# Moving the last pair's products ahead of the first inverse's products, and the bonus product to ScalarE, in a four-layer streaming encoder

## The chip, the core and the metric

The kernel runs on one core of a Trainium2 chip. A core has a matrix engine (TensorE, PE in the profile; its weight loads are shown as PEld), a vector engine (VectorE, DVE), an activation engine (ScalarE, ACT), a general engine (GpSimd, POOL) and a queue engine (SyncE, SP). Each takes its instructions in order from a queue of its own, and they wait for one another through semaphores. Matrix products land in PSUM, eight banks of 128 x 512 fp32; everything else lives in SBUF. The metric is the device time of one execution in microseconds (us).

## The reference, cut to what matters

Two residual layers, each followed by a gated convolutional FFN. The first mixes tokens by spatial gating, the second by an RWKV-7 recurrence. The change lies in the second mixer alone.

```
D, S, H, N = 1024, 512, 16 heads, 64 per head
r, k, v = xr @ w_r, xk @ w_k, xv @ w_v            # 512 x 1024 each
g = sigmoid(xg @ g1) @ g2
y = wkv7_scan(r, decay, k, v, -kk, kk * a)         # S_t = S diag(w) + (S a) b^T + v k^T ; y_t = S_t r_t
y = groupnorm_per_head(y) * ln_w + ln_b
bonus = sum(r * k * r_k, per head) * v
out = ((y + bonus) * g) @ w_o
```

The recurrence is computed in chunks of 64 positions. Inside a chunk it needs the inverse of a unit triangular 64 x 64 matrix for each head.

## The kernel before, in words

Activations lie as [128 channels, 512 positions] tiles, eight of them for the 1024 channels. A dense product with a 1024 x 1024 weight runs in fp32r with operands split into a high and a low part: three matmuls of 128 x 512 for each pair of a weight tile and an input tile (`mm3`, lines 325 to 327). `dense_steps` gives two input tiles, that is six matmuls, between two yields.

The heads come as eight **pairs** p = 0 to 7 of 128 channels, in two **groups** of four. Pairs 0 to 3 are group 0, pairs 4 to 7 group 1. `rwkv_main` consists of Python generators that emit instructions a bit at a time, and `weave` interleaves them:

- `pairs()` is the main stream of the first half. For each pair it emits `decay` (two pairs ahead), `operands` (one pair ahead) and `products`. `products` multiplies the pair's operands chunk by chunk into banks `aux` and `us` (L973, two halves; L988), VectorE masks them (L977), ScalarE copies parts into `ti` (L978) and `bt` (L991). A pair takes three main steps.
- `invert(g)` inverts the triangular blocks of a group. It copies and transposes them (ScalarE L1046 or VectorE L1044, VectorE L1051), runs a chain of 30 elimination steps j on VectorE (L1062 to L1070, each step on the result of the one before), transposes back (L1051 twice), and joins the blocks by small 32 x 32 matmuls (L1090, L1093) into bank `e` (group 0) or `aux` (group 1), which ScalarE copies out (L1098, L1103, L1105). It has 25 yields: one after the first transposes, fifteen in the chain, one after the transposes back, eight among the matmuls.
- `fill` is the stream of matrix work that keeps TensorE busy: `projections()` (keys, then values V0 to V7, four dense steps each), `gates()`, `project()` (the output product, first with group 0, then with group 1).
- `scan(g)` is the main stream of the second half: eight chunks of group g, three main steps each (L1301/L1305, L1314, L1321/L1326), whose matmuls wait for VectorE copies and sums between them. `finish` normalises what two chunks gave (ScalarE square L1342, VectorE L1347, GpSimd power L389, VectorE L1357, transposes by TensorE L1363, VectorE L1366).

The value stream is what the change touches most. After the four dense steps of pair m, ScalarE copies the bank to tile `v` (L854; one buffer). During the dense steps of pair m + 1, `value(m, v)` emits the centring transposes (L868) and later the **bonus**: a matmul of r*k with ones scaled by r_k (L883) into a bank, VectorE multiplies that bank by `v` into `rt` (L885), ScalarE adds the bias `ln_b` in place (L886). While pairs are still running, the dense accumulators, the transposes and the bonus share tag `mm`, which has two banks.

`weave(main, side, fill, rate, lag, side_rate)` takes one main step after another; after each it adds `side_rate` to the side's account and `rate` to the fill's, and takes as many whole steps of each as are due. A fill step may be issued no earlier than TensorE's last instruction of `lag` main steps ago. The order of the work is that of emission, with a planner that lays out each engine's queue ahead of time: among instructions that it takes to be ready, the one emitted first goes first. VectorE's elimination steps are tied to nothing but their operands, so they are put wherever VectorE is free; the inverse's matmuls are tied behind the last TensorE instruction (`step`).

Lines 1422 to 1440 set the order of the stretch around the change: pairs 0 to 3 with fill; pairs 4, 5, 6 with `invert(0)` at 2.2 steps a main step and fill at 1.9 (nine main steps; 19 side and 17 fill steps, and one more fill step inside `invert(0)`, L1077); then the last two main steps of pair 7 with `invert(0)` at 2.2 and fill at 1.2 (4 side, 2 fill steps); then what is left of `invert(0)` (one yield), with a fill step and a step of `ahead = invert(1)` for each yield; one fill step; `scan(0)` with the rest of `invert(1)` at 1.15 and fill at 0.66; `scan(1)` with fill at 0.72; and a written-out end (lines 1444 to 1454).

`gates()` takes `idle()` steps, two matmuls on constants (L1124) whose result nobody reads, as fill until group 0's last chunks are normalised (`normed`, L1177); two of them are taken in `scan(1)`. `gate` multiplies the finished `rt` by the gate in PSUM (L1209), and splits the result into the operands of the output product (L1213, L1214). After the last main step of `scan(1)` four dense steps of group 0's output product are left, m = 6 and 7; they lie among the normalisation of the last chunks, the gate's products (L1201) and the transposes L1363, ahead of the first product with group 1.

Of the kernel before, what the change touches and what calls it, by code (L numbers as in the profile page):

```python
# [12 lines left out]
F32 = mybir.dt.float32  # L13
F32R = mybir.dt.float32r
AF = mybir.ActivationFunctionType
ALU = mybir.AluOpType
# [4 lines left out]
P = 128  # L21
D = 1024
KT = 8
T = 512
# [5 lines left out]
GN_EPS = 64e-5  # L30
C1 = -0.5 * math.exp(-0.5)

RATES = ((1.9, 2), (1.9, 6, 2.2), (0.66, 2, 1.15), (0.72, 2), (1.2, 6, 2.2))
LEAD = 1
WB = 4
FIRST0, WAIT, STEPS = 1, 1, (2, 2, 2, 2)
# [108 lines left out]
class Emit:  # L145
# [622 lines left out]
    def rwkv_main(self, r, ctx, gain):  # L768
        nc, tc, A = self.nc, self.tc, self.A
        V, S, G = nc.vector, nc.scalar, nc.gpsimd  # L770
# [5 lines left out]
        ip = r.ip  # L776
# [31 lines left out]
        def projections():  # L808

            load = Ahead([lambda n=n, m=m: self.parts(n, m) for n in PARTS for m in range(KT)])  # L810

            def key(m, a):
                while m >= NKEY and m - NKEY not in used:
                    yield
                ks[m] = tmp("key", NKEY, T)
                S.copy(ks[m], a)

            for m in range(KT - 2):
                a = self.acc("mm")
                yield from self.dense_steps(a, load.take(), r.xk)  # L820
                yield from key(m, a)
                yield

            ws = [load.take(), load.take(False)]
            accs = [self.acc("mm") for _ in range(2)]
            xv = []
            for k in range(KT):
                for j in range(2):
                    self.mm3(accs[j], self.wcols(ws[j], k * P, P), r.xk[k], k == 0, k == KT - 1)
                while len(xv) < min(k + 3, KT):  # L830
                    xv.append(r.mix(3, len(xv)))
                if k == 4:
                    load.fetch()
                yield
            for j in range(2):
                yield from key(KT - 2 + j, accs[j])
            late = iter(())
            for m in range(KT):
                a = self.acc("mm")
                w = load.take()  # L840
                if m == KT - 2:
                    ga["w"] = load_gate(0)
                for n, _ in enumerate(self.dense_steps(a, w, xv)):
                    yield
                    next(late, None)
                    if m == KT - 1 and n == 0:
                        gw[0] = gate_weights(ga["w"])
                        ga["parts"] = self.gate_parts()
                    if m == KT - 1 and len(gx) < 2:
                        gx.append(gate_mix(len(gx)))  # L850
                for _ in late:
                    yield
                v = ip.tile([P, T], F32, tag="v", bufs=1, name=self.uid("v"))
                S.copy(v, a)  # L854
                late = value(m, v)
            next(late)
            tail.append(late)

        def value(m, v):
            g, i = divmod(m, 4)  # L860

            def bank():
                return self.acc("mm" if len(done) < KT else "aux")

            vt = ip.tile([P, NCH, C], F32, tag="vt", bufs=1, name=self.uid("vt"))
            q = bank()
            for b in range(4):
                nc.tensor.matmul(q[:, b * P:(b + 1) * P], v[:, b * P:(b + 1) * P], self.c("center", P),  # L868
                                 start=True, stop=True)
            q4 = q.rearrange("p (b h f) -> p b h f", b=4, h=2)  # L870
            for hd in range(2):
                for par in range(2):
                    S.copy(vt[H[1 - hd], par::2, :], q4[H[par], :, hd, :])
            nc.sync.dma_start(vtd[:, :, m].rearrange("c p f -> p c f"), vt)
            yield
            yield

            while m not in done:
                yield
            wb = ip.tile([P, P], F32, tag="wb", bufs=1, name=self.uid("wb"))  # L880
            S.activation(wb, self.c("bones", P), AF.Copy, scale=self.p("r_k", m))
            q = bank()
            nc.tensor.matmul(q, wb, rt[g][:, i, :], start=True, stop=True)  # L883
            b = rt[g][:, i, :]
            V.tensor_tensor(b, q, v, ALU.mult)  # L885
            S.activation(b, b, AF.Identity, bias=self.p("ln_b", m))  # L886
            vdone.add(m)
            yield

# [137 lines left out]
        def invert(g):  # L1027
# [21 lines left out]
            def turn(out, src):  # L1049
                for bs in [slice(n, n + 8) for n in range(0, 32, 8)] if g == 1 else [slice(0, 32)]:  # L1050
                    V.transpose(out[:, bs], src[:, bs])  # L1051
# [6 lines left out]
            for j in range(1, 31):  # L1058
# [6 lines left out]
                else:  # L1065
                    a = tt[:, j, j + 1:32].unsqueeze(1).to_broadcast([P, j, ni])
                    b = tt[:, 0:j, j].unsqueeze(2).to_broadcast([P, j, ni])
                    q = pr[:, 0:ni * j].rearrange("p (c i) -> p c i", i=ni)
# [7 lines left out]
            if g == 0:  # L1076
                next(fill)  # L1077
            turn(y.rearrange("p u t -> p t u"), tt.rearrange("p s t -> p t s"))
            yield
            off, own = blocks("off"), iter(Q)  # L1080
            for i in range(2):
                for hf in range(2):
                    ps = self.acc("aux" if g == 1 else "e").rearrange("p (u t) -> p u t", t=32)
                    us = slice(16 * hf, 16 * hf + 16)
                    for u in range(16):
                        for hd in range(2):
                            b0, b1 = Q[2 * hd][0], Q[2 * hd + 1][0]
                            n = 16 * hf + u
# [15 lines left out]
                        else:  # L1104
                            S.copy(tg[b0, us, 32:64], ps[b0])  # L1105

        gx, tail = [], []

        def gate_mix(k):
            with ExitStack() as behind:  # L1110
# [92 lines left out]
        def gate(g, i, ts, q=None):  # L1203

            if q is None:
                q = self.acc("aux")[:, 0:ts.stop - ts.start]
                opening(g, i, ts, q)
            o = rt[g][:, i, ts]
            V.tensor_tensor(o, o, q, ALU.mult)  # L1209
            while len(outs[g]) <= i:  # L1210
                outs[g].append(tuple(self.xr.tile([P, T], F32R, tag=t, bufs=10, name=self.uid(t)) for t in ("mxh", "mxl")))
            oh, ol = (x[:, ts] for x in outs[g][i])
            S.copy(oh, o)  # L1213
            V.tensor_tensor(ol, o, oh.bitcast(F32), ALU.subtract)  # L1214
# [202 lines left out]


        fill = itertools.chain(projections(), gates(), project())
        gw, ga = {}, {}  # L1420
        main = pairs()
        self.weave(until(main, lambda: 3 in done), None, fill, *RATES[0], ktiles=STEPS[0])
        inv = invert(0)
        for _ in take(inv, FIRST0):
            pass
        self.weave(until(main, lambda: KT - 2 in done), inv, fill, *RATES[1], ktiles=STEPS[1])
        load(0, 0)
        ahead = invert(1)
        next(ahead)
        self.weave(main, inv, fill, *RATES[4], ktiles=STEPS[1])  # L1430
        for _ in inv:
            next(fill)
            self.step(ahead, (mybir.EngineType.PE,))
        ctx.close()
        ep = ctx.enter_context(tc.tile_pool(name="scan", bufs=1))
        inv = ahead
        r.sg = [ep.tile([P, T], F32R, name=f"sg{i}") for i in range(3)]
        for _ in range(LEAD):
            next(fill, None)
        self.weave(scan(0), inv, fill, *RATES[2], ktiles=STEPS[2])  # L1440
        for _ in inv:
            pass
        self.weave(scan(1, left.pop()), None, fill, *RATES[3], ktiles=STEPS[3])
        rest, left = left.pop(), None
# [80 lines left out]
```

## Time and profile before

| | us |
|---|---|
| three runs, median (lowest to highest) | 1244.08 (1243.03 to 1244.97) |
| the profiled execution, own time | 1245.55 |
| its span, first to last instruction | 1243.7 |
| TensorE busy in it | 1226.8 |
| VectorE busy in it | 851.1 |
| ScalarE busy in it | 633.1 |
| mean granted TensorE clock | 0.996 |

The profile is of one execution. The span is shorter than the execution's own time by what lies around the first and the last instruction. Busy times say how long an engine had an instruction in it; matmuls are pipelined, so each matmul's time overlaps the next one's, and a TensorE that is busy throughout may still run at a lower clock. A time followed by an engine and a line is the start of an instruction counted from the span's start, then its duration; square brackets give the idle time of the engine just before it, and who ended that.

### The profile page before, as it was taken

How to read it: one execution, taken by the hardware profiler on the slowest of the kernel's cores; microseconds unless marked ns; L12 is line 12 of the kernel's file. 1: busy time of each engine (PE TensorE's matmuls, PEld its weight loads, DVE VectorE, ACT ScalarE, POOL GpSimd, SP SyncE). 2: the span in 40 equal slices, each digit the busy share in tenths (PEclk: the TensorE clock that was granted, in tenths of full speed). 3: DMA queues.
4: the chain of work that ended last, by engine and by line, in shares of the span. 5: the costliest groups of instructions: out<-in, count | busy, mean ns of one | idle time of the engine just before them, and what ended most of it. 6: DMA issues, size and time to landing. Idle time of an engine off the chain costs nothing.

```text
span 1243.7 us, 19411 instructions
## 1 busy us (share of the span) xinstructions
PE 1226.8 (99%) x7535; PEld 1000.2 (80%) x7535; DVE 851.1 (68%) x1418; ACT 633.1 (51%) x1089; POOL 81.4 (7%) x106
## 2 busy tenths in 40 slices
PE   9999999999999999999999999999999999999997
PEld 6878888888888888877887777778888888888886
DVE  5566578888876454675899698776777777872323
ACT  6544455555554343466787667424544444543232
POOL 1100200000000001000000013222000000000000
PEclk9999999999999999999999899999999999999999
DMA  7232457887556776326888797654223223333332
GB/s 273 94 105 82 132 180 246 246 249 241 192 172 193 220 226 196 109 81 182 220 242 237 188 280 233 219 171 135 85 102 102 90 97 102 97 88 104 97 93 81
DMA packets 125133, 201.65 MB, mean 162 GB/s; under 512 B 39857, under 2 KB 63153, under 8 KB 125041
## 3 DMA queue, kind: packets, MB, share of 16 engines
q10 hardware_dynamic: 38976, 112.87, 29.5%
q1 hardware_dynamic: 86064, 87.54, 22.6%
q8 instruction: 59, 0.97, 0.3%
q14 instruction: 34, 0.27, 0.1%
HBM read 152.93 MB, written 47.45 MB: 161 GB/s over the span
## 4 chain that ended last, share of the span: by engine, by line
PE 91%; DVE 4%; DMA 3%; ACT 1%; issue 0%; SPq 0%; POOL 0%; DVEq 0%; POOLq 0%; ACTq 0%
PE mm L325 9%; PE mm L327 9%; PE mm L326 9%; PE aux L325 6%; PE aux L326 6%; PE aux L327 6%; PE e L325 6%; PE e L326 6%; PE us L325 6%; PE e L327 6%; PE us L327 6%; PE us L326 6%; PE us L1314 1%; PE aux L973 1%; PE aux L988 1%; PE us L1321 1%
## 5 line engine op out<-in xcount | busy, mean ns | idle before, releaser
L237 ACT CAST w<-w 128x512 fp32r<-128x512 f32 x340 | 206.5, 611 | 359.8 <-PE aux L327 92.6
L238 DVE TENSOR_TENSOR w<-w,w 128x512 fp32r<-128x512 f32 x340 | 230.5, 680 | 180.2 <-ACT w L237 179.6
L325 PE MATMUL mm<-mxh,w 128*128 128x512 f32 x408 | 167.9, 412 | 2.7 <-DVE rt L885 2.6
L327 PE MATMUL mm<-mxh,w 128*128 128x512 f32 x408 | 161.1, 395 | 0.0
L326 PE MATMUL mm<-mxl,w 128*128 128x512 f32 x408 | 160.6, 394 | 0.0
L325 PEld LDWEIGHTS mm<-mxh,w 128*128 128x128 f32 x408 | 77.0, 189 | 22.8 <-DVE rt L885 3.3
L327 PEld LDWEIGHTS mm<-mxh,w 128*128 128x128 f32 x408 | 77.0, 189 | 17.1 <-issue 0.8
L326 PEld LDWEIGHTS mm<-mxl,w 128*128 128x128 f32 x408 | 77.1, 189 | 16.2 <-issue 1.7
L575 ACT ACTIVATE cv<-z,par 128x512 f32<-128x512 f32 x88 | 71.7, 817 | 26.5 <-DVE z L573 21.2
L325 PE MATMUL aux<-mxh,w 128*128 128x512 f32 x216 | 84.5, 391 | 0.0
L325 PE MATMUL us<-mxh,w 128*128 128x512 f32 x216 | 84.5, 391 | 0.0
L327 PE MATMUL aux<-mxh,w 128*128 128x512 f32 x216 | 84.2, 390 | 0.0
L326 PE MATMUL aux<-mxl,w 128*128 128x512 f32 x216 | 84.1, 389 | 0.0
L326 PE MATMUL us<-mxl,w 128*128 128x512 f32 x216 | 84.1, 389 | 0.0
L327 PE MATMUL us<-mxh,w 128*128 128x512 f32 x216 | 84.1, 389 | 0.0
L354 POOL TENSOR_TENSOR ss<-ss,sq 128x512 f32<-128x512 f32 x24 | 31.7, 1323 | 761.1 <-ACT sq L352 761.1
L325 PE MATMUL e<-mxh,w 128*128 128x512 f32 x208 | 81.4, 391 | 0.0
L326 PE MATMUL e<-mxl,w 128*128 128x512 f32 x208 | 81.1, 390 | 0.0
L327 PE MATMUL e<-mxh,w 128*128 128x512 f32 x208 | 81.0, 389 | 0.0
L576 DVE SCALAR_TENSOR_TENSOR cv<-z,par,cv 128x512 f32<-128x512 f32 x88 | 66.0, 752 | 19.5 <-ACT cv L575 19.5
L577 DVE SCALAR_TENSOR_TENSOR cv<-z,par,cv 128x512 f32<-128x512 f32 x88 | 66.0, 752 | 2.9
L325 PEld LDWEIGHTS aux<-mxh,w 128*128 128x128 f32 x216 | 40.5, 188 | 9.0 <-issue 0.5
(1113 smaller groups left out, 2555.2 us busy)
## 6 DMA issues: line engine op xcount, KB each, us to landing
w<-in_wup ACTq DMA_DIRECT2D x88, 512.0 KB, 3.7
w<-in_wdn ACTq DMA_DIRECT2D x32, 512.0 KB, 3.7
st<-std SPq DMA_DIRECT2D x15, 640.0 KB, 6.6
w<-wkd ACTq DMA_DIRECT2D x16, 512.0 KB, 5.1
w<-wvd ACTq DMA_DIRECT2D x16, 512.0 KB, 5.1
w<-wod ACTq DMA_DIRECT2D x16, 512.0 KB, 4.2
w<-in_wdn ACTq DMA_DIRECT2D x16, 384.0 KB, 3.3
w<-in_wsu ACTq DMA_DIRECT2D x8, 512.0 KB, 3.7
```

The source lines that it names most:

```text
L237: nc.scalar.copy(hi[r, :n], src)
L238: (lo_eng or nc.vector).tensor_tensor(lo[r, :n], src, hi[r, :n].bitcast(F32), ALU.subtract)
L325: mm(acc, wh, xh, start=first, stop=False)
L326: mm(acc, wh, xl, start=False, stop=False)
L327: mm(acc, wl, xh, start=False, stop=last)
L354: nc.gpsimd.tensor_tensor(self.ss, self.ss, self.sq, ALU.add)
L575: nc.scalar.activation(c, z[:, 2:], AF.Identity, scale=cw(2, i), bias=self.p("conv_b", l * 44 + i))
L576: nc.vector.scalar_tensor_tensor(c, z[:, 1:T + 1], cw(1, i), c, ALU.mult, ALU.add)
L577: nc.vector.scalar_tensor_tensor(c, z[:, 0:T], cw(0, i), c, ALU.mult, ALU.add)
L973: nc.tensor.matmul(qs[hd][:, c - ch.start, :], bk[H[hd], c, C * hd:C * hd + P], ar[H[hd], c, :], start=True, stop=True)
L988: nc.tensor.matmul(qs[hd][:, c, :], bk[H[hd], c, C * hd:C * hd + P], dg[H[hd], c, :], start=True, stop=True)
L1314: nc.tensor.matmul((us, ux)[hd][H[hd], 1, i, :], ti[g][H[hd], i, c, :], wt[H[hd], i, :], start=True, stop=True)
```

## The change

- `RATES[1]`, the weave of pairs 4 to 6: `invert(0)` gets 1.6 steps a main step (was 2.2).
- `RATES[4]`, the weave of pair 7's last two main steps: no side stream (was `invert(0)` at 2.2).
- What is left of `invert(0)` is then stepped in a loop; from the step that emits its transposes back (`turned`) on, each step is followed by a step of `invert(1)`, and on every second one a fill step comes first.
- The bonus: ScalarE copies the bank into `rt`; VectorE multiplies `rt` by `v` there, both in SBUF. The bias `ln_b` is added in `gate`, where VectorE's multiplication becomes (rt + ln_b) * gate in one instruction.
- Tile `v` has two buffers (was one).

```
-RATES = ((1.9, 2), (1.9, 6, 2.2), (0.66, 2, 1.15), (0.72, 2), (1.2, 6, 2.2))
+RATES = ((1.9, 2), (1.9, 6, 1.6), (0.66, 2, 1.15), (0.72, 2), (1.2, 6))
...
-                v = ip.tile([P, T], F32, tag="v", bufs=1, name=self.uid("v"))
+                v = ip.tile([P, T], F32, tag="v", bufs=2, name=self.uid("v"))
...
-            V.tensor_tensor(b, q, v, ALU.mult)
-            S.activation(b, b, AF.Identity, bias=self.p("ln_b", m))
+            S.copy(b, q)
+            V.tensor_tensor(b, b, v, ALU.mult)
...
             turn(y.rearrange("p u t -> p t u"), tt.rearrange("p s t -> p t s"))
+            turned.append(g)
             yield
...
-        gx, tail = [], []
+        gx, tail, turned = [], [], []
...
-            V.tensor_tensor(o, o, q, ALU.mult)
+            V.scalar_tensor_tensor(o, o, self.p("ln_b", 4 * g + i), q, ALU.add, ALU.mult)
...
-        self.weave(main, inv, fill, *RATES[4], ktiles=STEPS[1])
-        for _ in inv:
-            next(fill)
-            self.step(ahead, (mybir.EngineType.PE,))
+        self.weave(main, None, fill, *RATES[4], ktiles=STEPS[1])
+        for n, _ in enumerate(inv):
+            if turned and n % 2 == 0:
+                next(fill)
+            if turned:
+                self.step(ahead, (mybir.EngineType.PE,))
```

## The prediction, made before the changed kernel was run

> **What bounds the kernel now.** The page comes first: engines, then the slices.
>
> ```profile
> span 1243.7 us, 19411 instructions
> ...
> PE 1226.8 (99%) x7535; PEld 1000.2 (80%) x7535; DVE 851.1 (68%) x1418; ACT 633.1 (51%) x1089; POOL 81.4 (7%) x106
> ...
> PEclk9999999999999999999999899999999999999999
> ```
>
> TensorE is busy for all but 1243.7 - 1226.8 = 16.9 us. The matrix work stays the same but for one item below, so the change can only move idle time and lost clock. Both show in one place, the slice whose clock reads 8. The list of TensorE's waits names it:
>
> ```profile
> PE mm L325 <- DVE rt L885: 2.6, 2, 2.3
> ...
> PE us L1314 <- DVE wt L1304: 1.0, 2, 0.8
> ...
> PE e L1090 <- DVE ix L1051: 0.2, 1, 0.2
> ```
>
> The columns are total, times, longest. The two waits for L885 are these:
>
> ```profile
> 684.11 0.50 PE L325 MATMUL mm<-mxh,w 128*128 128x512 f32 x1 [0.35 <-DVE rt L885]
> ...
> 692.30 1.02 PE L883 MATMUL mm<-rt,wb 128*128 128x512 f32 x2
> ...
> 694.31 0.40 PE L327 MATMUL mm<-mxh,w 128*128 128x512 f32 x1
> ...
> 696.99 0.50 PE L325 MATMUL mm<-mxh,w 128*128 128x512 f32 x1 [2.28 <-DVE rt L885]
> ```
>
> The bonus of pair 2 ends before 693.4, but VectorE empties its bank only at 696.25, and the first dense matmul of V4 wants a bank of the same tag. Behind this gap the clock falls; the stretches below give TensorE's busy time, and the granted clock as the third number from the end:
>
> ```profile
> 696.00:697.00 1.00, 0.01 (x1) 0.02 (x1) 0.96 (x4) 0.03 (x1) 0.00 (x0) 1.00 1.14 324
> 697.00:698.00 1.00, 1.00 (x4) 0.84 (x5) 0.90 (x4) 1.00 (x2) 0.00 (x0) 0.98 0.85 252
> 698.00:699.00 1.00, 1.00 (x4) 0.76 (x3) 1.00 (x1) 0.89 (x2) 0.00 (x0) 0.50 0.34 100
> ...
> 703.00:704.00 1.00, 1.00 (x4) 0.79 (x3) 0.00 (x0) 0.98 (x3) 0.00 (x0) 0.50 0.00 0
> 704.00:705.00 1.00, 1.00 (x5) 0.76 (x4) 0.00 (x0) 0.97 (x2) 0.00 (x0) 0.60 0.01 1
> 705.00:706.00 1.00, 1.00 (x6) 0.74 (x4) 0.00 (x0) 0.99 (x2) 0.00 (x0) 1.00 1.03 215
> ```
>
> Six stretches from 698 to 704 stand at 0.50, one at 0.60, one at 0.98: 3.0 + 0.4 + 0.02 = **3.4 us of lost clock**. The place costs 0.35 + 2.28 + 3.4 = 6.0 us, and 0.2 for L1090.
>
> **The bonus and the second buffer of `v`.** Why was L885 late? VectorE's and ScalarE's timelines:
>
> ```profile
> 691.93 0.68 DVE L977 TENSOR_TENSOR lq<-aux,cst 128x512 f32<-128x512 f32 x1
> ...
> 692.77 0.68 DVE L977 TENSOR_TENSOR lq<-us,cst 128x512 f32<-128x512 f32 x1
> ...
> 696.25 0.68 DVE L885 TENSOR_TENSOR rt<-mm,v 128x512 f32<-128x512 f32 x1
> ```
>
> ```profile
> 681.31 0.40 ACT L881 ACTIVATE wb<-cst,par 128x128 f32<-128x128 f32 x1 [2.19 <-PE mm L883]
> ...
> 693.49 0.40 ACT L978 COPY ti<-lq 64x256 f32<-64x256 f32 x1 [0.44 <-DVE lq L977]
> 693.91 0.59 ACT L991 COPY bt<-aux 128x512 f32<-128x512 f32 x1
> 694.40 0.59 ACT L991 COPY bt<-us 128x512 f32<-128x512 f32 x1
> ```
>
> VectorE works off elimination steps between pair work and runs late: the matmuls that the first L977 masks had ended by 689.2, 2.7 us before it.
>
> ```profile
> 688.87 0.27 PE L973 MATMUL aux<-ar,bk 64*128 64x128 f32 x1
> ```
>
> ScalarE has gaps. The new copy is of L854's kind:
>
> ```profile
> L854 ACT COPY v<-mm x8: 562/586/587, 658.2 to 755.3; 128x512 f32<-128x512 f32 x8
> L886 ACT ACTIVATE rt<-rt,par x8: 711/724/727, 671.1 to 761.2; 128x512 f32<-128x512 f32 x8
> ```
>
> So 8 x 0.59 us replace 8 x 0.72 on ScalarE. VectorE's eight multiplications keep 0.69: L953, SBUF alone, takes that too.
>
> ```profile
> L953 DVE TENSOR_TENSOR ss<-ss,key 128x512 f32<-128x512 f32 x2 | 1.4, 689 | 0.0
> ```
>
> Pair 1's copy finds ScalarE free at 681.31: the 0.35 us go. Pair 2's copy is not free of VectorE, since ScalarE's queue is in order. Behind it wait v's copy and with it the transposes. If it stands behind both L991, which stand behind L978 and so behind L977, it runs from 694.99 to 695.58; TensorE is free from about 694.54 (694.31 plus one matmul interval of 0.23), or 694.2 with the 0.35 gained: a gap of 1.0 to 1.4. If it goes ahead of them, none is left. Below nothing it can't go; the upper end is the old 2.28, if queues shift so that it is later still. I take 0.7: **-1.6**. With the second `v` buffer v's copy no longer waits for the multiplication; that adds no gain of its own, as the same bank wait covered it.
>
> The page's clock row has one digit below 9, and it follows the one gap above 2 us; the 0.8 us ahead of L1314 left none. At 0.7 to 1.4 I expect no drop: **-3.4**. The Trainium skill, "TensorE: Matmul & The Clock Gate", section "HAM oscillation — how this bites in real kernels", gives as a rule that TensorE must not idle for more than about 3.4 us, or its clock halves. By that rule no gap of 2 to 3 us costs clock, and rival (1) below would fall away. The trace differs: 2.28 us of idle sufficed here, so I keep that rival.
>
> **The rates and the order.** Before, pair 7's products stood behind the inverse's transposes, and VectorE then had nothing to do:
>
> ```profile
> 707.48 0.69 DVE L977 TENSOR_TENSOR lq<-aux,cst 128x512 f32<-128x512 f32 x1 [6.00 <-issue]
> ```
>
> The elimination steps filled every free place of VectorE. Now the first inverse's emission ends at step j = 27 when pair 6 ends (1 + 14 yields, was 20), and pair 7 with two fill steps comes ahead of j = 28 and the transposes back. Their VectorE time stays; its cover is the TensorE work of V4, pair 7's products and three steps of V5 (seven dense steps of 1.4 us alone give 10), so L1090's 0.2 us wait goes: **-0.2**. If that cover failed, VectorE's two transposes, 2.0 us each, would be the price.
>
> The fill counts change. Ahead of `scan(0)`, from pair 4 on, there were 17 + 1 + 2 + 1 steps; now 17 + 1 + 2 + 4. `scan(0)` starts with V6.3 done instead of V6.0, and with nine more steps of `invert(1)` emitted. The same work lies earlier, with its DMAs through ACT's queue: no gain or loss by itself, as long as TensorE is full. Two ends follow.
>
> First, the fill reaches `idle()` three steps earlier, so three idle steps are taken instead of two:
>
> ```profile
> 792.74 1.13 PE L1124 MATMUL e<-cst 128*128 128x256 f32 x4
> 793.83 0.69 PE L1321 MATMUL us<-vu,cbt 128*64 128x64 f32 x16
> ```
>
> One step occupies 793.83 - 792.74: **+1.1**. TensorE is full there, nothing hides it.
>
> Second, the end of `scan(1)` keeps two dense steps of group 0 (m = 7) instead of four. The end before:
>
> ```profile
> 839.55 0.69 PE L1326 MATMUL e<-vu,st 128*64 128x64 f32 x16
> 840.17 0.50 PE L325 MATMUL mm<-mxh,w 128*128 128x512 f32 x1
> ...
> 843.02 0.28 PE L325 MATMUL us<-sg,gwh 128*128 128x256 f32 x1
> ...
> 846.35 0.60 PE L1363 MATMUL aux<-cst,y 128*128 128x128 f32 x4
> 846.70 0.48 PE L325 MATMUL mm<-mxh,w 128*128 128x512 f32 x1
> ...
> 848.17 0.49 PE L325 MATMUL mm<-mxh,w 128*128 128x512 f32 x1
> ```
>
> ```profile
> 842.70 1.63 POOL L389 TENSOR_TENSOR gr<-rs,mhalf 128x8 f32<-128x8 f32 x1 [8.22 <-DVE rs L388]
> ```
>
> ```profile
> 844.58 0.69 DVE L1357 TENSOR_TENSOR y<-y,gr 128x512 f32<-128x512 f32 x1
> ...
> 846.58 0.49 DVE L1214 TENSOR_TENSOR mxl<-rt,mxh 128x128 fp32r<-128x128 f32 x2
> 846.98 0.61 DVE L1366 SCALAR_TENSOR_TENSOR rt<-aux,par,rt 128x128 f32<-128x128 f32 x2
> ```
>
> Two steps take 843.02 - 840.17 = 2.85 us, and all four stood under the chain from L1326 over GpSimd to L1366 and the first product with group 1 at 848.17. Two are gone from there: 2.85 us of idle at most. At least 1.75, as the transposes could start at 845.27, when L1357 ends, 1.1 sooner. But L1366 also stood behind VectorE's own L1214 (846.58 + 0.49), which isn't earlier. I take **+2.5**. The gate's new form costs what L1366 (0.33 at 128 wide) does against L1209 (0.28): about 0.05 x 4 on that chain, **+0.2**.
>
> Sum against the span: -0.35 - 1.6 - 3.4 - 0.2 + 1.1 + 2.5 + 0.2 = -1.75. I give 0.3 back for small waits in the scan: -1.5. The profiled execution's own time, 1245.55, is its span and 1.85 around it, and stands 1.5 above the median of the runs; the difference is carried over to that median: 1244.08 - 1.5 = **1242.6**.
>
> **Rivals.** (1) *The late gap drops the clock.* It is as long as the one that did. Against it: it is cut in two by the transposes' 0.35 us. At half clock for half to all of the 6.8 us seen, 1.7 to 3.4: 1244.3 to 1246.0. (2) *The copy is ahead of L991 and the late chain shortens.* Gap 0, late idle 1.75, no clock lost: -0.7 - 0.75 more, and VectorE, 7 us ahead with the second inverse, saves up to 1 of the scan's waits (1.0 for L1304): 1240.1 to 1241.1. For it: ScalarE's free stretches; less elimination ahead of L977. (3) *Slower: ScalarE's copy is held by VectorE.* L978 waits for a VectorE that is late, the copy behind it; the gap stays near 2 us, the clock drops as before. Then only 0.35 + 0.2 and at most 0.3 are gained and 3.8 lost: 1244.08 + 3.0 = 1247.1. It decides from a gap of about 2 us on; for it: L977 started 2.7 us after its matmuls, as shown. (4) *The edit misses:* V4 waits for v's copy instead, same queue, same size as the forecast.
>
> **How the numbers follow.** About 0.2% (2.5 us) is what a measurement can tell from no change: faster is below 1241.6, slower above 1246.6. Forecast 0.30, (1) 0.20, (2) 0.28, (3) 0.18, (4) 0.04. Faster: (2) and the forecast's lower edge, 0.31. Slower: (3) and (1)'s upper edge, 0.20. The rest, 0.49, is within. The range, 1239.2 to 1247.4, takes in the bounds of the two unknown gaps; it leaves out what lies beyond the far ends of (2) and (3), new waits that no row shows.
>
> **What would show it.** Right: no wait for L885, the wait ahead of V4 under 1.5 us and named after ScalarE; clock 1.00 from 690 to 710; three rows of four L1124 matmuls instead of two; an idle stretch of 1.75 to 2.85 us before the first product with group 1. Wrong: the clock at 0.50 anywhere, VectorE waits of more than 1 us at the start of `scan(0)`, or no idle at the end of `scan(1)`.

## The result, and the profile after

The changed kernel takes 1255.61 us, the median of four runs, 1255.22 to 1256.97; the kernel before takes 1244.53 on the same chip. The ratio goes by the single runs and is not the quotient of the two medians, 1.0089; it is 1.0093, 95% interval [1.0076, 1.0111]: **slower by some 11 us**, where 1242.6 was forecast and the range ended at 1247.4. The profiled execution has a span of 1253.4 us, 9.7 above that of before. One execution of a run below, e10, took 2038.86 us at a mean clock of 0.555; it is left out of that run's numbers. Lines from L1079 on have moved by one (L1193 is now L1194); L885 is now ScalarE's copy and L886 VectorE's multiplication.

The page of the changed kernel, span, engines and clock by slice:

```profile
span 1253.4 us, 19424 instructions
...
PE 1230.4 (98%) x7539; PEld 1001.8 (80%) x7539; DVE 852.4 (68%) x1418; ACT 631.8 (50%) x1089; POOL 83.3 (7%) x106
...
PEclk9999999999999999999999999998999999999999
```

The 8 has moved from the pairs to the late end, and TensorE has four matmuls more (7539, was 7535): one idle step, whose two matmuls in the program show as four in the trace. The list of its waits, total, times and longest:

```profile
PE mm L325 <- ACT rt L885: 3.1, 2, 2.5
PE mm L325 <- ACT mxh L1214: 2.3, 1, 2.3
PE mm L325 <- DVE h L1194: 1.7, 1, 1.7
PE us L1302 <- PE e L1327: 1.5, 2, 1.0
```

The wait for L885 has changed its engine and hardly its size (3.1 us in all, was 2.6); the other three waits are new. Where they lie shows in three stretches of the two kernels, before and then after. The first two numbers are the stretch's length and TensorE's busy time, so that their difference is its idle time:

```profile
580.00:700.00 120.00, 115.96 (x945) 93.25 (x943) 108.08 (x214) 84.57 (x162) 1.40 (x9) 0.99 0.85 231
700.00:790.00 90.00, 87.87 (x1474) 67.77 (x1471) 70.75 (x163) 63.34 (x120) 18.47 (x23) 0.97 0.77 235
790.00:880.00 90.00, 89.44 (x858) 70.68 (x855) 60.14 (x127) 32.66 (x69) 24.95 (x28) 1.00 0.47 155
```

```profile
580.00:700.00 120.00, 115.44 (x930) 92.46 (x925) 107.22 (x213) 86.69 (x165) 1.40 (x9) 0.99 0.83 231
700.00:790.00 90.00, 87.01 (x1433) 66.47 (x1431) 71.14 (x161) 60.34 (x115) 18.11 (x22) 0.99 0.76 235
790.00:880.00 90.00, 84.57 (x858) 66.10 (x858) 56.24 (x123) 30.02 (x65) 24.19 (x26) 0.96 0.47 147
```

Idle before: 4.04, 2.13, 0.56. Idle after: 4.56, 2.99, 5.43. So 0.5 us are lost in the pairs, 0.9 in the first scan, and **4.9 at the late end**.

**The gap ahead of V4.** ScalarE's timeline of the changed kernel (start, duration, instruction):

```profile
692.89 0.41 ACT L978 COPY ti<-lq 64x256 f32<-64x256 f32 x1 [3.25 <-DVE lq L977]
693.33 0.83 ACT L1046 COPY ix<-ti 32x768 f32<-32x768 f32 x1
694.18 0.40 ACT L978 COPY ti<-lq 64x256 f32<-64x256 f32 x1
694.61 0.59 ACT L991 COPY bt<-aux 128x512 f32<-128x512 f32 x1
695.09 0.59 ACT L991 COPY bt<-us 128x512 f32<-128x512 f32 x1
695.71 1.68 ACT L1046 COPY ix<-ti 32x768 f32<-32x768 f32 x2
...
697.41 0.59 ACT L885 COPY rt<-mm 128x512 f32<-128x512 f32 x1
```

The bonus's copy stands behind both L991, as the prediction had it, and also behind three copies L1046 of 0.83 us each: 2.5 us. These are the second inverse's blocks, which the reorder has brought here: in the kernel before the first of them ran behind the bonus.

```profile
698.06 0.83 ACT L1046 COPY ix<-ti 32x768 f32<-32x768 f32 x1
```

Without them the copy would have run from about 694.9 (an estimate, 697.41 - 2.5), the place that the prediction took as its late case. TensorE's row shows what it cost:

```profile
698.05 0.80 PE L325 MATMUL mm<-mxh,w 128*128 128x512 f32 x1 [2.54 <-ACT rt L885]
```

**The late end.** Three idle steps of four matmuls each are taken, two of them in one piece and one in two:

```profile
786.84 1.03 PE L1125 MATMUL e<-cst 128*128 128x256 f32 x4
789.49 0.70 PE L1125 MATMUL e<-cst 128*128 128x256 f32 x2
790.73 0.70 PE L1125 MATMUL e<-cst 128*128 128x256 f32 x2
793.86 1.13 PE L1125 MATMUL e<-cst 128*128 128x256 f32 x4
```

Then TensorE waits for an addition that empties a bank. VectorE's timeline, and TensorE's:

```profile
811.00 1.10 DVE L1358 TENSOR_TENSOR y<-y,gr 128x512 f32<-128x512 f32 x1 [1.03 <-POOL gr L389]
812.13 1.00 DVE L258 TENSOR_TENSOR gw<-w,gw 32x512 fp32r<-32x512 f32 x1
813.16 0.69 DVE L238 TENSOR_TENSOR gwl<-w,gwh 128x512 fp32r<-128x512 f32 x1
813.88 0.69 DVE L1194 TENSOR_TENSOR h<-h,mm 128x512 f32<-128x512 f32 x1
```

```profile
814.62 0.50 PE L325 MATMUL mm<-mxh,w 128*128 128x512 f32 x1 [1.67 <-DVE h L1194]
...
852.64 0.63 PE L1364 MATMUL aux<-cst,y 128*128 128x128 f32 x4 [0.44 <-DVE y L1358]
855.58 1.22 PE L325 MATMUL mm<-mxh,w 128*128 128x512 f32 x2 [2.31 <-ACT mxh L1214]
```

In the kernel before, VectorE's addition started 0.5 us sooner, behind the same L258 and L238, and nobody waited for it. The row of VectorE, then that of the same product on TensorE:

```profile
813.39 0.69 DVE L1193 TENSOR_TENSOR h<-h,mm 128x512 f32<-128x512 f32 x1
```

```profile
814.29 0.40 PE L325 MATMUL mm<-mxh,w 128*128 128x512 f32 x1
```

In the changed kernel TensorE is ready for this product at 812.95 (814.62 - 1.67), 1.3 us sooner than before. So the wait is made by both, VectorE 0.5 us later and TensorE 1.3 us sooner, and mainly by TensorE. The last two rows of TensorE are the end of `scan(1)`: 0.44 + 2.31 = 2.75 us of idle ahead of the first product with group 1.

**The clock.** The granted clock, third from the end, in stretches of 1 us:

```profile
697.00:698.00 1.00, 0.00 (x0) 0.00 (x0) 0.64 (x3) 0.98 (x2) 0.00 (x0) 0.96 0.97 290
698.00:699.00 1.00, 0.95 (x2) 0.84 (x3) 0.93 (x3) 0.95 (x3) 0.00 (x0) 0.50 0.77 175
...
700.00:701.00 1.00, 1.00 (x5) 0.81 (x4) 1.00 (x1) 0.00 (x0) 0.00 (x0) 0.50 0.63 242
701.00:702.00 1.00, 1.00 (x9) 1.00 (x9) 1.00 (x2) 0.00 (x0) 0.00 (x0) 0.83 0.00 0
...
855.00:856.00 1.00, 0.42 (x1) 0.42 (x2) 1.00 (x5) 0.56 (x2) 0.00 (x0) 0.50 0.00 0
...
860.00:861.00 1.00, 1.00 (x4) 0.80 (x3) 0.00 (x0) 0.00 (x0) 0.00 (x0) 0.50 0.00 0
861.00:862.00 1.00, 1.00 (x5) 0.76 (x4) 0.47 (x1) 0.00 (x0) 0.00 (x0) 0.62 0.00 0
```

Behind V4's gap three stretches at 0.50 and one at 0.83 lose 1.7 us (3.4 before). Behind the late gap six at 0.50, the first of them half in the gap itself, and one at 0.62 lose 3.4, where none were lost before. Together: idle +6.3, the third idle step +1.1, clock +1.7 make 9.1 of the 9.7 us; the rest isn't located.

### The profile page after: what moved, and what is told of

Same layout as the page of the kernel before. It is cut to its first block, busy times and chain, and to the rows that moved or that the text cites. A ratio compares the mean times of both kernels' runs of the same rounds, so it can differ in the third digit from the quotient of the medians.

```text
span 1253.4 us, 19424 instructions
## 1 busy us (share of the span) xinstructions
PE 1230.4 (98%) x7539; PEld 1001.8 (80%) x7539; DVE 852.4 (68%) x1418; ACT 631.8 (50%) x1089; POOL 83.3 (7%) x106
## 4 chain that ended last, share of the span: by engine, by line
PE 89%; DVE 6%; ACT 2%; DMA 1%; issue 1%; POOL 0%; DVEq 0%; POOLq 0%; SPq 0%; ACTq 0%
PE mm L325 9%; PE mm L327 9%; PE mm L326 9%; PE aux L325 6%; PE aux L327 6%; PE aux L326 6%; PE e L325 6%; PE us L325 6%; PE e L326 6%; PE e L327 6%; PE us L327 6%; PE us L326 6%; DVE pr L1069 1%; DVE li L1070 1%; PE aux L973 1%; PE aux L988 1%
## 5 line engine op out<-in xcount | busy, mean ns | idle before, releaser
L238 DVE TENSOR_TENSOR w<-w,w 128x512 fp32r<-128x512 f32 x340 | 230.6, 680 | 180.7 <-ACT w L237 180.3
```

Of the source, the lines that this page charges most:

```text
L238: (lo_eng or nc.vector).tensor_tensor(lo[r, :n], src, hi[r, :n].bitcast(F32), ALU.subtract)
```

## The experiments

Theory: the dense steps are a fixed budget of cover. The reorder spends three more of them ahead of `scan(0)`, and they are missing at the late end. Rivals: the loss belongs to the bonus's and the gate's new forms, or to the gap ahead of V4 and its clock. "Idle" stands for TensorE's idle time in the three stretches above, from one profile of each kernel.

```
                            us       ratio, 95% interval       idle 580-700, 700-790, 790-880
before                      1244.5   1                         4.0   2.1   0.6
after                       1255.6   1.0093 [1.0076, 1.0111]   4.6   3.0   5.4
e1_fill_as_before           1256.9   1.0090 [1.0068, 1.0111]   5.6   6.4   3.6
e2_bonus_alone              1248.2   1.0021 [1.0009, 1.0034]   4.7   4.3   1.7
e3_order_alone              1253.7   1.0062 [1.0039, 1.0085]   4.6   3.5   5.1
e4_blocks_behind_bonus      1256.8   1.0090 [1.0066, 1.0115]   1.9   6.5   5.4
e5_scan0_fewer_fill         1253.7   1.0071 [1.0053, 1.0089]   4.5   6.5   1.4
e6_scan1_fewer_fill         1251.1   1.0047 [1.0032, 1.0062]   4.6   4.0   4.1
e7_constants_in_late_gap    1253.3   1.0064 [1.0048, 1.0080]   4.6   3.0   3.7
e8_before_fill_three_on     1253.6   1.0063 [1.0045, 1.0081]   4.6   2.2   5.1
e9_gate_bias_alone          1250.4   1.0045 [1.0031, 1.0059]   5.1   4.0   1.7
e10_fewer_eliminations      1255.9   1.0077 [1.0053, 1.0100]   5.6   1.8   5.4
e11_fill_ends_as_before     1252.3   1.0059 [1.0046, 1.0071]   4.6   3.0   2.9
e12_constants_ahead_of_v4   1251.7   1.0060 [1.0047, 1.0072]   3.2   7.6   0.6
e13_order_fill_as_before    1249.7   1.0035 [1.0022, 1.0048]   4.8   5.1   1.8
e14_copy_and_buffers        1247.3   1.0020 [1.0010, 1.0031]   4.9   4.0   0.6
e15_lead_0                  1249.8   1.0038 [1.0025, 1.0051]   3.9   3.4   4.1
e16_lead_2                  1247.9   1.0016 [1.0003, 1.0030]   3.9   3.2   2.0
```

In e1, e3, e8, e9, e10, e13 and e14, 0.3 to 1.3 us of the first idle number is a wait for a DMA near 589 us, ahead of everything that the edits touch; the other profiles don't have it. So differences of about 1 us in that column mean nothing for these runs.

None of them beats the kernel before. The ratios go by runs of the kernel before on the same chip; its median varied from 1244.4 to 1245.5.

### Which part: the order or the bonus

**e1_fill_as_before**, the changed kernel with one fill step in the loop, as before:

```
-            if turned and n % 2 == 0:
+            if turned and n == 2:
```

> The changed kernel, but its loop behind pair 7 takes one fill step instead of four, as many as before. Theory A (the loss comes from the fill standing three steps further on): two idle steps again (-1.1 us), no 1.7 us wait for the sum L1194 (-1.7), four dense steps left at the end of scan(1), so no gap there (-2.75) and no drop of the clock behind it (-3.4): about 1255.6 - 8.9 = 1246.7, give or take 1.5, since the inverse's small matmuls may then wait up to 2 us for ScalarE's copies. Rival B (the loss comes from VectorE having no rest ahead of the scan, or from ScalarE's copy and the longer gate instruction): no more than 3 us of it goes, 1252.6 or above.

The time is that of the changed kernel, in rival B's range, while the late end does what theory A said: no wait for L1194, two idle steps, 0.95 us ahead of group 1 and no clock lost there. But the small matmuls of the inverse now stand open. TensorE's timeline:

```profile
728.80 1.06 PE L1094 MATMUL e<-li,off 32*32 32x32 f32 x33 [3.01 <-issue]
```

The profile names nothing that TensorE waited for here; in the changed kernel this wait is 0.61. The clock fell behind this gap too, and 6.4 us are idle between 700 and 790. So the fill steps of the loop aren't surplus: they cover the inverse's matmuls, and taking them back wins nothing.

**e2_bonus_alone**, the kernel before with the bonus, the gate and the buffer of `v` as in the change, and **e3_order_alone**, the changed kernel with these three as before (the edit of e2 is shown; that of e3 takes the same lines the other way):

```
-                v = ip.tile([P, T], F32, tag="v", bufs=1, name=self.uid("v"))
+                v = ip.tile([P, T], F32, tag="v", bufs=2, name=self.uid("v"))
...
-            V.tensor_tensor(b, q, v, ALU.mult)
-            S.activation(b, b, AF.Identity, bias=self.p("ln_b", m))
+            S.copy(b, q)
+            V.tensor_tensor(b, b, v, ALU.mult)
...
-            V.tensor_tensor(o, o, q, ALU.mult)
+            V.scalar_tensor_tensor(o, o, self.p("ln_b", 4 * g + i), q, ALU.add, ALU.mult)
```

> The kernel before with the bonus on ScalarE, two buffers of v and the bias in the gate; rates and order as before. Theory A: no fill step is shifted, so none of the late losses; ahead of V4 the copy stands behind both L991 with no copy of the second inverse's blocks in front, a gap of 1.0 to 1.4 us instead of 2.3, and no drop of the clock (3.4 us): 1244.5 - 0.35 - 1.1 - 3.4 + 0.2 = 1239.9, between 1238.5 and 1241.5. Rival B (ScalarE's copy is held by VectorE just as long, or the longer gate instruction costs on the late chain): gap of 2 us or more and the clock at 0.50 behind it, 1244 to 1245.5.

> The changed rates and order with the bonus, the gate and v's one buffer as before. Theory A: all late losses are there (9 us), the gap ahead of V4 is VectorE's L885 again, about 2.3 us, with 1.7 to 3.4 us of clock: 1254 to 1258. Rival B (the bonus on ScalarE and the gate's form carry the loss): 1250 or below.

The order makes most of the loss (1.0062 alone) and the bonus part a smaller one (1.0021). e2's time is above both ranges that were given for it. Run alone, the bonus part has the gap that the prediction foresaw, 1.26 us, and no idle time is won by it, since the next wait takes over. TensorE's timeline of e2:

```profile
695.88 0.50 PE L325 MATMUL mm<-mxh,w 128*128 128x512 f32 x1 [1.26 <-ACT rt L885]
699.97 0.69 PE L1090 MATMUL e<-ix,ti 32*32 32x32 f32 x32 [2.22 <-DVE ix L1051]
...
851.32 0.50 PE L325 MATMUL mm<-mxh,w 128*128 128x512 f32 x1 [0.95 <-ACT mxh L1213]
```

1.26 + 2.22 is more than the 2.28 + 0.19 of before. In e3 the place costs 1.62 (VectorE's L885) + 0.78 (v's copy). So neither half alone makes the gap of 2.54 us: in e2 the first L1046 stands behind the copy (at 696.63), and in e3 they stand ahead (from 693.06) but the bank doesn't wait for ScalarE. Its late waits are those of the changed kernel but for 0.12 and 0.19 less in the last two, 0.32 and 2.12: so much the gate's form adds there.

**e4_blocks_behind_bonus**, the changed kernel with the second inverse's first blocks tied behind ScalarE's last instruction:

```
-        next(ahead)
+        with tc.issue_after(self.last(mybir.EngineType.Activation)):
+            next(ahead)
```

> The changed kernel, but the copies of the second inverse's blocks (L1046) are tied behind ScalarE's last instruction at that point, so that none stands ahead of pair 2's bonus copy. Theory A: the gap ahead of V4 falls from 2.54 us to what L978 and L991 leave, 0.9 to 1.1, and the clock stays at 1.00 there (1.7 us): 1255.6 - 1.5 - 1.7 = 1252.4, give or take 1; the late losses stay. Rival B (the copy is held by VectorE's masks whatever stands between): gap above 2 us, 1255 to 1256.

The gap ahead of V4 is gone, so the L1046 in ScalarE's queue did make it. The time is not better (the profiled execution took 1253.8 us, the other three 1256.7 to 1258.0): 2.7 us less idle ahead of 700, 3.5 more behind it. TensorE's timeline:

```profile
703.15 1.12 PE L883 MATMUL mm<-rt,wb 128*128 128x512 f32 x2 [1.44 <-ACT vt L873]
710.90 1.16 PE L868 MATMUL mm<-cst,v 128*128 128x128 f32 x8 [0.82 <-ACT v L854]
...
734.32 0.68 PE L1315 MATMUL us<-wt,ti 64*64 64x64 f32 x16 [2.54 <-DVE wt L1305]
```

**e10_fewer_eliminations** takes VectorE work out of both inverses; it leaves out 14 of the 30 elimination steps, so what it computes isn't the encoder any more:

```
+                if 16 <= j < 30:
+                    if j % 2 == 1:
+                        yield
+                    continue
```

> The changed kernel; part of the computation is left out: elimination steps 16 to 29 of both inverses, which is VectorE work alone. Theory A (between pair 2 and the end of the first inverse VectorE sets the pace, so gaps move and don't go): the waits ahead of V4 (2.5 us) and in the first inverse shrink to under 1 us together and the front clock drop goes, while the late waits (1.7 us for the h addition, 2.3 us ahead of group 1) stay; time 1249 to 1253 us. Theory B (ScalarE's queue alone makes the gap ahead of V4): that gap stays at 2 us or more, since the block copies are as many as before.

The gap ahead of V4 stays, 2.46 us after ScalarE: theory B, its queue makes it and not VectorE's load. The 0.48 us for L1305 at the start of `scan(0)` are gone, and the late waits are as in the changed kernel.

### Where the fill stands

**e8_before_fill_three_on**, the kernel before with three fill steps more ahead of `scan(0)`, and nothing else of the change:

```
-LEAD = 1
+LEAD = 4
```

> The kernel before with four fill steps instead of one ahead of scan(0) and nothing else changed. Theory A (three fill steps further on is enough for the late losses): three idle steps (+1.1), the wait for L1194 (+1.7), the gap at the end of scan(1) (+2.3 to 2.75) and, where the clock drops, 1.7 to 3.4 behind it: +5 to +9, 1249.5 to 1253.5. Rival B (the reordered first half or the bonus on ScalarE bring them): within 2 us of the kernel before, no gap at the end.

This alone reproduces the late end of the changed kernel: three idle steps, a wait of 0.99 us behind L1326, and in TensorE's timeline

```profile
813.62 0.50 PE L325 MATMUL mm<-mxh,w 128*128 128x512 f32 x1 [1.67 <-DVE h L1193]
853.05 0.63 PE L1363 MATMUL aux<-cst,y 128*128 128x128 f32 x4 [0.32 <-DVE y L1357]
855.81 1.22 PE L325 MATMUL mm<-mxh,w 128*128 128x512 f32 x2 [2.12 <-ACT mxh L1213]
```

The late idle time is 5.1 us, 0.6 in the kernel before, and 1.7 us of clock are lost behind each of the first and the last of these waits. The ratio 1.0063 against 1.0093 makes the shift of the fill the largest part of the change that was run by itself; e3, which holds it too, has 1.0062.

**e16_lead_2** and **e15_lead_0** set the same number to 2 and to 0:

> The kernel before with one fill step more ahead of scan(0). Theory A (by the number of steps: a third of what three steps gave): a third idle step at most (+1.1 us) or a late idle stretch of 0.5 to 1 us; no wait of 1.67 us for the h addition; 1245 to 1248 us. Theory B (layout, not number): late end as in the kernel before, waits of 3 us or more between 700 and 800 us; 1247 to 1251 us.

> The kernel before with one fill step less ahead of scan(0). Theory A (the fill's place counts by its number of steps): one idle step instead of two (-1.1 us), one dense step more at the end of scan(1), where it adds nothing; new waits at the start of scan(0) up to 1 us; 1242.5 to 1244.5 us. Theory B (the planner's layout of the scan changes with any shift and the kernel before has a lucky one): waits of 3 us or more between 700 and 800 us, 1247 to 1251 us.

One step more gives two idle steps, 1.33 us ahead of group 1 and no wait for the addition: theory A at the late end, by the number of steps, if somewhat above its bound; but the 3.2 us idle between 700 and 790 (2.1 in the kernel before) go with theory B. One step less goes with theory B too, by its time and by 3.4 us idle there; two idle steps are taken, where theory A had one, and at the late end a wait of 1.93 us is new for which the profile names no releaser. So each theory has part of it: a late end that goes by the number of steps from 1 to 4, and a scan that is laid out anew each time. With 1.0038, 1, 1.0016 and 1.0063 for 0, 1, 2 and 4 the kernel before stands at the bottom.

**e5_scan0_fewer_fill, e6_scan1_fewer_fill** and **e11_fill_ends_as_before** take the steps back from the changed kernel elsewhere: a lower rate in `scan(0)`, a lower rate in `scan(1)`, or none in pair 7's last steps and one less ahead of `scan(0)`:

```
-RATES = ((1.9, 2), (1.9, 6, 1.6), (0.66, 2, 1.15), (0.72, 2), (1.2, 6))
+RATES = ((1.9, 2), (1.9, 6, 1.6), (0.54, 2, 1.15), (0.72, 2), (1.2, 6))    e5
+RATES = ((1.9, 2), (1.9, 6, 1.6), (0.66, 2, 1.15), (0.64, 2), (1.2, 6))    e6
+RATES = ((1.9, 2), (1.9, 6, 1.6), (0.66, 2, 1.15), (0.72, 2), (0.4, 6))    e11, with LEAD = 0
```

> The changed kernel with fill at 0.54 instead of 0.66 a main step in scan(0): 12 fill steps there instead of 15, so that scan(1) starts with the fill where it stood before. Theory A (the late losses come from the fill's place): two idle steps, no wait for L1194, no gap at the end of scan(1); minus 1.1 + 1.7 + 2.75 and the clock there (1.7 to 3.4), plus new gaps in scan(0), where three dense steps of 1.4 us are missing as cover, up to 4: 1247 to 1251. Rival B (they come from the reordered first half): 1253 or above, with the same gaps at the end.

> The changed kernel with fill at 0.64 instead of 0.72 a main step in scan(1): 15 fill steps instead of 17, so that four dense steps of group 0 are left at its end, as before; the three idle steps stay. Theory A: the gap of 2.3 + 0.4 us ahead of the first product with group 1 goes, and with it any drop of the clock there: minus 2.75 and minus 1.7 to 3.4, plus gaps in scan(1) of at most 2.7: 1250 to 1253. Rival B: the gap stays, since the chain over GpSimd and VectorE sets it whatever TensorE has to do: 1255 or above.

> The changed kernel with no matrix fill in the last two main steps of pair 7 and one step less ahead of scan(0), so that scan(0) begins with V6.0 done as in the kernel before, while the inverse keeps its four fill steps. Theory (the late losses come from where the fill stands when scan(0) begins; the cover of the inverse from the steps taken there): two idle steps, no wait for the h addition, a wait of about 0.9 us ahead of group 1 from the gate's form; the front as in the changed kernel, with about 1 to 3 us of new waits where the three steps are missing; 1247 to 1251 us. Rival (late losses belong to the order of the inverses and not to the fill): 1.7 us for the h addition and 2.3 ahead of group 1 stay; 1254 to 1257 us.

In e5 and e11 the wait for the addition goes, two idle steps are left, and 0.95 us stand ahead of group 1. The steps are then missing where they were taken. In e5 it is mainly one place, in TensorE's timeline:

```profile
770.94 1.12 PE L1327 MATMUL e<-vu,st 128*64 128x64 f32 x16 [3.19 <-issue]
```

The clock fell behind it. So e5's time is in rival B's range, with most of theory A's late end. e6 spreads the loss best and has lost no clock in its profile. Its time is in theory A's range, but the gap that should have gone keeps 1.71 us ahead of group 1, and 1.11 for L1358 are new. e11 did at the late end what the theory said, and its time is 1.3 us above the range given; idle is 3.8 us above that of before in all.

**e7_constants_in_late_gap** leaves the gap's cause and fills it, with two more idle steps ahead of the first product with group 1:

```
+        for _ in range(2):
+            with tc.issue_after(self.last(mybir.EngineType.PE)):
+                idle()
```

> The changed kernel with two more idle steps (four matmuls on constants, 2.2 us) between the last transposes and the first product with group 1, where TensorE waited 2.3 us. The wait itself stays filled, so no time is gained by it; if the clock drops for TensorE's idle time (theory A), it stays at 1.00 behind the gap, and the times of all runs lie 1.7 to 3.4 us lower, 1252 to 1254, and closer together. If the drop has another cause, 1255 to 1257 as before.

The wait there fell to 0.58 us, no clock was lost behind it, and the ratio is 1.0064 where the changed kernel has 1.0093. The mean clock of its four runs is .996 to .999, that of the changed kernel's .993 to .994, so the late gap's price in clock isn't the profile's alone.

### The gate's form, the bare order, and the clock

**e9_gate_bias_alone** (the kernel before without the bias on ScalarE, with the gate's new form) and **e14_copy_and_buffers** (e2 with bias and gate as before):

> The kernel before with one part of the change: the bias on ScalarE after the bonus is dropped and the gate's multiplication adds it. Theory (the gate's form costs more than the 0.2 us that the prediction took, because it stands twice in the late chain ahead of the first product with group 1): that wait, of which the kernel before shows nothing over 0.3 us, becomes about 0.9, as in the run with the bonus part alone; the pairs and the inverse stay as before, time +0.5 to +1.5 us. Rival (the late wait of that run came from elsewhere, such as the copy or the second buffer): no wait there over 0.4 us, time as before within 0.3.

> The kernel before with ScalarE's copy of the bonus and the second buffer of v; the bias stays on ScalarE and the gate as it was. Theory A (the gate's form makes the late wait of 0.95 us in the run of the whole bonus part): that wait is gone; the gap ahead of V4 is 1.0 to 1.6 us after ScalarE; 1244 to 1247 us. Rival (the late wait comes from the copy): 0.9 us ahead of group 1 as there, 1247 to 1249 us.

The 0.95 us ahead of group 1 are there in e9 and e2 and not in e14, so they are the gate's form; late idle 1.7, 1.7 and 0.6. e9's time missed its range by 4 us: idle grew by 1.9 us between 700 and 790 as well, with one wait of 2.33 ahead of L1320, and clock was lost twice. In e14 the front is much as in e2: 1.27 ahead of V4, then 1.54 for v's copy.

**e13_order_fill_as_before**, e11 with the old bonus, gate and buffer, has of the change the order alone:

> The changed kernel with the old bonus, the old gate and one v buffer, and with the fill as in the run before this that begins scan(0) at V6.0: of the change only the order of the inverses' ends and pair 7 is left. Theory A (the remainder of 7 us is the bonus's and the gate's new forms): late end as in the kernel before, no wait over 0.5 us ahead of group 1, two idle steps; 1245 to 1247 us. Theory B (the planner's new layout of the scan costs several us whatever the edit is): new waits of 3 us or more in all between 700 and 800 us that stand at other lines than in the changed kernel; 1248 to 1252 us.

Theory B by its time and its waits: no clock lost, no wait ahead of group 1, but 5.1 us idle between 700 and 790 in small pieces. Some of them from TensorE's timeline:

```profile
751.03 0.69 PE L1091 MATMUL aux<-ix,ti 32*32 32x32 f32 x32 [0.74 <-DVE ix L1051]
763.64 1.16 PE L868 MATMUL aux<-cst,v 128*128 128x128 f32 x8 [0.65 <-ACT v L854]
768.28 1.12 PE L883 MATMUL aux<-rt,wb 128*128 128x512 f32 x2 [0.45 <-ACT wb L881]
```

**e12_constants_ahead_of_v4**, four matmuls on constants in the kernel before, between V3 and V4, to hold the clock:

```
+                if m == 4:
+                    q = self.acc("e")
+                    with tc.issue_after(self.last(mybir.EngineType.PE)):
+                        for _ in range(4):
+                            nc.tensor.matmul(q[:, 0:256], self.c("ident", P), self.cst[:, 0:256], start=True, stop=True)
```

> The kernel before with four matmuls on constants (128x256, 1.1 us in all) between V3 and V4, in the gap of 2.3 us. Theory (the gap makes the clock drop by chance, in about half of the executions or more, at 1.7 to 3.4 us each): with about 1.2 us of idle left the clock stays at full in every execution, mean clock .999 in every run, time 1.0 to 3.4 us below the kernel before, 1241 to 1243.5. Rival (the matmuls delay V4 and nothing is gained, or the drop comes without the gap): the same time within 0.5 us, and the clock below .998 in some runs.

The four matmuls took 1.9 us, not the 1.1 expected. The gap fell to 0.57 us and the clock held there. But 33 us later there is a wait that the kernel before doesn't have, and 3.4 us of clock are lost behind it. ScalarE's timeline and TensorE's:

```profile
724.65 0.62 ACT L256 CAST gw<-w 32x512 fp32r<-32x512 f32 x1 [5.70 <-DMA btd<-bt]
...
728.66 0.59 ACT L859 COPY v<-mm 128x512 f32<-128x512 f32 x1
```

```profile
729.30 1.22 PE L873 MATMUL aux<-cst,v 128*128 128x128 f32 x4 [4.60 <-ACT v L859]
```

ScalarE's queue is laid out otherwise here: the casts of the gate's weights stand ahead of v's copy, and behind it in the kernel before. The casts wait 5.70 us, by the profile for a DMA, and the copy with them. Both the theory and the rival fell; what the clock alone is worth is left open.

## Why the prediction was wrong

Its terms against the two traces, in us against the kernel before:

| step | predicted | measured |
|---|---|---|
| wait of V3 | -0.35 | -0.35, and a new 0.52 at V2 |
| gap ahead of V4 | -1.6 | +0.26 (2.28 to 2.54) |
| clock behind it | -3.4 | -1.7 in this execution |
| wait for L1090 | -0.2 | -0.2 |
| third idle step | +1.1 | +1.1 |
| gap ahead of group 1 | +2.5 | +2.75 with the gate's form |
| gate's form | +0.2 | +0.3 here (e3), 1.1 in the order of before (e14 to e2) |
| clock behind the late gap | 0; rival (1) 1.7 to 3.4 | +3.4 |
| shift of the fill, else | 0 | +1.67 for L1194, +0.99 for L1302 |
| small waits in the scan | +0.3 | +0.9 |

**The step that failed first** is the sentence on the shifted fill: "The same work lies earlier, with its DMAs through ACT's queue: no gain or loss by itself, as long as TensorE is full." Its two ends were named and rightly sized (three idle steps; 2.75 us in bounds of 1.75 to 2.85). What the sentence called nothing was a loss of 1.67 + 0.99 us in `scan(1)`, not counting the clock: the same products come sooner on TensorE, so that it reaches one before VectorE has emptied its bank. e8 shows it, since with the shift alone in the kernel before the same 1.67, 0.99 and 2.12 us come up.

**The second** is the gap ahead of V4, taken as 0.7 in bounds of 0 to 2.28 and measured as 2.54, outside them. The queue behind which the copy stands was read from the trace of before, without the instructions that the reorder itself brings into it, the L1046 of `invert(1)`. These copies belong to its first step, which stands at the same place in both programs, so the edit doesn't show that they move. The prediction counts "nine more steps" of this inverse and asks nowhere for their place on ScalarE. The outcome is rival (3)'s, a gap near 2 us, by another instruction than the one that it named; e4 and e10 show that it is these. Even with 0.7 little idle time would have been won, as e2, e4 and e14 show: behind this gap the next wait is for VectorE's transposes or for ScalarE's copies.

**The third** is the clock. Rival (1) was right about its price: the late gap lost 3.4 us. It stood at 0.20, and rivals (1) and (3) were priced as if only one could happen. Both happened; with the waits that no row showed, this took the time beyond the range. By size this is the largest miss: of the 13.0 us between forecast and result the rows above explain 10.8, and 5.1 of them are clock, 2.7 the shift, 1.9 the gap ahead of V4 and 1.1 small waits. The half of the 3.4 us ahead that did go, -1.7, is luck: it went behind a longer gap, not a shorter one.

Right were the third idle step, V3's wait, the gap at the end of `scan(1)`, L1090's wait and, in the order of the change, the gate's form.

What stays open: the parts don't add up. e8 (1.0063), e13 (1.0035) and e2 (1.0021) sum to 1.0119, above the whole change at 1.0093. The shift is enough for the late waits (e8). The wait for the addition and that of over 2 us ahead of group 1 go with it (e1, e5, e11, e13), but no run that took it back came to the time of the kernel before; in each, idle time came up elsewhere. Some edits lay out queues far behind them anew (e12, e15), and the waits that this brings were not separated from those of the edit itself.

## What to carry to other kernels

Where an engine is 99% busy, the dense work that lies around the waits is a budget: a reorder that spends it earlier has to be charged at the place where it will be missing, wait by wait, and not only at the last one. Before a copy is moved to another engine, write out that engine's queue as it will be, with what the same change moves into it. And when a gap is closed, look for the wait that stands right behind it: here it was 2.22 us in e2, 1.44 in e4 and 1.54 in e14.

## What the runs showed of the hardware

The same gap did or didn't cost clock. V4's gap of 2.28 us lost 3.4 us in the profile of before and in e16, and 1.7 in e15; 2.53 in e6 and 2.50 in e7 lost none; the late gap of 2.31 lost 3.4 in the changed kernel and none in e4. Shorter gaps close together did it as well: 1.27, 1.54 and 0.43 within 5 us in e14 lost 3.4, while 1.62 and 0.78 in e13 lost none. A gap of 1.67 lost 1.7 in e4 and e8 and none in the changed kernel and e3. The losses between 560 and 880 us come in steps of about 1.7 us in all these profiles, and gaps of 1.5 to 3 us are better priced here as a chance of one or two such steps than by a threshold. The Trainium skill, "TensorE: Matmul & The Clock Gate", section "HAM oscillation — how this bites in real kernels", has idle of more than about 3.4 us as the limit. In the rows of this paragraph that lost clock less was enough.

The kernel before itself ran at mean clocks of .995 to .999 and 1243.0 to 1250.5 us, so an effect below 2 us needs many runs.
